# Low parts of weight chunks 7 to 41: a negating copy on ScalarE and an accumulating DMA from GpSimd, for every second chunk of both mixes

## The chip, the core and the metric

The kernel runs on one core of a Trainium2 chip. The time is that of one execution on the device in microseconds; of several runs the median is given. The engines are TensorE (PE in the profile), VectorE (DVE), ScalarE (ACT), GpSimd (POOL) and SyncE (SP, which here only issues DMAs). Each engine works through its own instructions in the order in which they stand; semaphores hold an instruction back until what it needs is done.

## The reference

A decoder trunk of two layers on 512 tokens of 1024 features, in fp32. Each layer is a token mix and a convolutional feed-forward block:

```python
def token_mix(h, ...):
    z = h @ w_in + b_in
    u_pool, u_conv, q, k, v, qi, ki, wi, gates = split_cols(z, IN_SIZES)
    ...
    y_pool = pool_mixer(u_pool, pool_w, pool_scale) @ w_pool_out
    y_conv = conformer_conv(u_conv, conv_dw_w, conv_dw_b, conv_ln_g, conv_ln_b, w_conv_out)
    y_attn = dsa_attention(q, k, v, qi, ki, wi) @ w_attn_out
    g = jax.nn.sigmoid(gates.astype(jnp.float32)).reshape(B, L, N_BRANCH, D_MODEL).astype(h.dtype)
    merged = g[:, :, 0] * y_pool + g[:, :, 1] * y_conv + g[:, :, 2] * y_attn
    return merged @ w_o

def reference(x, positions, ...):
    h = layer_norm(x, ln_in_g, ln_in_b)
    for l in range(DEPTH):
        mix = token_mix(h, positions, w_in[l], ...)
        h = layer_norm(DEEPNORM_ALPHA * h + mix, ln1_g[l], ln1_b[l])
        ffn = conv_ffn(h, w_up[l], ffn_dw_w[l], ffn_dw_b[l], w_down[l])
        h = layer_norm(DEEPNORM_ALPHA * h + ffn, ln2_g[l], ln2_b[l])
    return h
```

The mix has three branches. The pooling branch averages over windows of 2 to 16 tokens. The convolution branch filters 256 channels with 31 taps over time. The attention branch has an indexer (eight heads of relu logits, summed with weights) that chooses 128 of the visible keys for each query, and then rotary attention over those.

## The kernel before

**Weights.** All weights come from DRAM as chunks of 128 partitions x 1024 fp32 (512 KB), 123 for each layer, in the order of use. A chunk is split into two fp32r numbers (fp32 rounded to the format that TensorE takes): `w_hi`, the rounded value, and `w_lo`, what is left. Activations are split in the same way. A product is then three matmuls into one bank: hi x hi (L289), lo of the activation (L290), lo of the weight (L291). A chunk of the input projection holds 8 blocks of 128 rows, so it is 24 matmuls of 512 columns.

`Weights.emit` makes a chunk: SyncE issues its DMA into `w_raw` (L70, two buffers), ScalarE rounds it into `w_hi` (L74), and VectorE subtracts, `w_lo` = raw - hi (L78). Of the chunks in `side` (24, 26 to 40 of each mix, and some elsewhere) GpSimd subtracts instead, in two halves. `w_hi` and `w_lo` have four buffers each. `take` hands out the next chunk, and has the chunks up to two further ones (`look`) made.

**The mix.** Chunks 0 to 2 of a layer belong to its head (indexer keys, attention keys, the first half of the pooling channels), 3 to 6 to the indexer's queries, 7 to the second half of the pooling channels, 8 to 11 to the convolution's input, 12 to the values, 13 to 16 to the attention queries, 17 to 44 to the gates and the outputs of pooling and convolution, 45 to 56 to the attention's output and the merged output. Chunks 57 to 122 are the feed-forward block's.

Beside the projections run generators, of which some steps are taken after each chunk: the indexer (`index_gen`), whose logits TensorE puts into the two banks `pb_s` (L475, L476), ScalarE empties them into one of three `u` (L478), and VectorE adds them up in `pb_v` (L483) and then finds the largest (L490, L491); the pooling (L516 to L526 on GpSimd, L528 to L531 on VectorE); and the convolution (`conv_gen`). The latter works in two halves of 128 channels. ScalarE scales 23 of a half's taps (L595, two buffers `cvt`), GpSimd adds each to `cv` (L596); VectorE does the other seven into a bank `pb_p` (L598, L601) and adds both at the end (L604), which also frees that bank. There are two `pb_p`; the projection of chunk 16 (attention query tile 3) takes one of them.

Rotary embedding (`rotate`, `swapped`) copies a tile on ScalarE (L413), swaps its quarters by four SyncE DMAs (L405), multiplies on GpSimd (L407) and adds on VectorE (L417). `stack` splits the result (L424 ScalarE, L112 VectorE).

The order of instructions on each engine is decided when the program is built, by a scheduler with its own estimate of durations; work that is marked `high_priority` is put ahead of other work that is ready at the same time. Engines then keep this order on the chip.

Of the kernel before, what the change touches and what calls it, by code (L numbers as in the profile page):

```python
# [11 lines left out]
AF = mybir.ActivationFunctionType  # L12
ALU = mybir.AluOpType
# [30 lines left out]
N_CHUNK = 123  # L44
NSPLIT = {"mix": 3, "ffn": 3}
LAG = 2
MIX_SIDE = range(24, 42, 2)
ISSUE_ORDER = mybir.DependencyInfo(mybir.DependencyClass.NoSync, mybir.DependencyReason.DATA)
SIDE = 4
LN_POOL = ()  # L50
# [4 lines left out]
class Weights:  # L55
    def __init__(self, tc, w, raw_pool, split_pool, look, nchunk):
        self.tc, self.nc, self.w = tc, tc.nc, w
        self.raw_pool, self.split_pool = raw_pool, split_pool
        self.look = look
        self.n = nchunk  # L60
        self.emitted = 0
        self.used = 0
        self.ready = []
        self.side = set()

    def emit(self, upto):
        nc = self.nc
        while self.emitted < min(upto, self.n):
            raw = self.raw_pool.tile([P, D], F32, name="w_raw", tag="w_raw")
            nc.sync.dma_start(out=raw, in_=self.w[self.emitted])  # L70
            hi = self.split_pool.tile([P, D], F32R, name="w_hi", tag="w_hi")
            lo = self.split_pool.tile([P, D], F32R, name="w_lo", tag="w_lo")
            with self.tc.high_priority():
                nc.scalar.activation(hi, raw, AF.Copy)  # L74
                eng = nc.gpsimd if self.emitted in self.side else nc.vector
                for c in range(2 if self.emitted in self.side else 1):
                    cs = slice(512 * c, 512 * c + 512) if self.emitted in self.side else slice(0, D)
                    eng.tensor_tensor(out=lo[:, cs], in0=raw[:, cs], in1=hi[:, cs].bitcast(F32),  # L78
                                      op=ALU.subtract)
            self.ready.append((hi, lo))  # L80
            self.emitted += 1

    def take(self, look=None):
        self.emit(self.used + 1 + (self.look if look is None else look))
        self.used += 1
        return self.ready.pop(0)

# [2 lines left out]
def trunk_kernel(ctx, tc, x, positions, w, poolw, params, lnv, cons, out):  # L90
    nc = tc.nc
# [9 lines left out]
    W = Weights(tc, w, raw_pool, split_pool, 2, DEPTH * N_CHUNK)  # L101
# [203 lines left out]
    def down_proj(nk, lhs, ln, head):  # L305
# [3 lines left out]
        for s in range(2):  # L309
# [11 lines left out]
            def finish(b):  # L321
                hv = h[:, b, s * 512:(s + 1) * 512]
                V.scalar_tensor_tensor(out=hv, in0=hv, scalar=ALPHA, in1=po[b],
                                       op0=ALU.mult, op1=ALU.add)
                norm.stats(b, s)
                if s == 1:
                    norm.apply(b)
# [11 lines left out]
            if nt:  # L339
                wts = [W.take(look=nt - 1 - i) for i in range(nt)]  # L340
                W.emit(W.used + 4 - nt)
                for b in range(NB):
                    for i in range(nt):
                        for a in range(2):
                            first = mm(b, wts[i], npair - nt + i, a)
                            if i == a == 0 and b >= LAG and norm.tr[b - LAG] is not None:
                                tc.add_manual_dep(first.ins, norm.tr[b - LAG].ins.name, ISSUE_ORDER)
                    finish(b)
# [6 lines left out]
    def mix(l, head, prev, ln, nxt):  # L355
        es = ExitStack()
        with es:
# [5 lines left out]
            def q_slot(tag, dt=F32R):  # L363
                return slot(tag, {"qa": 6, "qb": 4, "qc": 4}[tag], dt)
# [7 lines left out]
            def p_slot(dt=F32):  # L372
                return slot("part", 9, dt, [P, 528])
# [9 lines left out]

            bga, bgb = [], []
            W.side.update(l * N_CHUNK + i for i in MIX_SIDE)

            def pump(q, n):
                while q and n > 0:
                    try:
                        n -= next(q[0])  # L390
                    except StopIteration:
                        q.pop(0)
# [366 lines left out]
            for jt in range(KT):  # L759
# [8 lines left out]
                hi, lo = q_slot("qa" if jt < 6 else "qb"), p_slot(F32R)[:, 0:L]  # L768
# [47 lines left out]
    for l in range(DEPTH):  # L816
        ffn_head = new_head("ffn")
        norm = mix(l, mix_head, norm, (1 + 2 * l, False), ffn_head)
        last = l == DEPTH - 1
        mix_head = None if last else new_head("mix")  # L820
        norm = ffn(l, ffn_head, norm, (2 + 2 * l, last), mix_head)
# [99 lines left out]
```

## Time and profile before

| | |
|---|---|
| median of 3 runs | 1506.07 us (1505.48 to 1506.64) |
| profiled execution | 1506.84 us, of which its span is 1505.0 us |
| mean granted TensorE clock | 0.994 |
| TensorE / VectorE / ScalarE / GpSimd busy | 97% / 63% / 45% / 35% |
| w_lo on VectorE (L78) | 210 times, 285.9 us |
| w_hi on ScalarE (L74) | 246 times, 260.6 us |
| w_lo halves on GpSimd (L78) | 72 times, 98.4 us |
| chain that ended last | TensorE 78%, GpSimd 8%, VectorE 6% of the span |

The profile is one execution, with the start and end of each instruction. The busy share of an engine is an average over the whole program; the mixes, the feed-forward blocks and the ends of the layers are loaded differently. The span runs from the first to the last instruction; 1.84 us of the execution lie outside it. In the rows "<-" behind an idle time names the instruction that released the waiting one.

### The profile page before, as it was taken

To read this page: it belongs to the slowest core of one execution; us is meant where nothing else is said; L and a number is where in the kernel's file an instruction comes from. 1 tells how busy PE (TensorE), PEld (TensorE's weight loads), DVE (VectorE), ACT (ScalarE), POOL (GpSimd) and SP (SyncE) were. 2 spreads that over 40 slices of the span, in tenths; PEclk is the share of its full clock that TensorE was granted. 3 is DMA by queue.
4 is the path that set the end of the run, shared out by engine and by line. 5 is a ranking of instruction groups with operands and counts; after the bars stand their busy time and mean duration, and the time that the engine had idled before them with its cause. 6 is when DMAs were issued, how large, how long until landed. Compare 5 with 4: busy or idle time off the path is not lost.

```text
span 1505.0 us, 18629 instructions
## 1 busy us (share of the span) xinstructions
PE 1454.7 (97%) x6850; PEld 1210.9 (80%) x6850; DVE 949.4 (63%) x1600; ACT 681.5 (45%) x1064; POOL 520.4 (35%) x395
## 2 busy tenths in 40 slices
PE   5998999999999999999999989999999999999997
PEld 5886888887878888888898768888878788888885
DVE  6789997645666555523267999865565655554234
ACT  5677455532544444421256874554235444443110
POOL 2458632237471111100134894220747311111004
PEclk9999999999999999999999999999999999999999
DMA  4432232232233333333224323222324333333331
GB/s 151 132 108 76 88 97 70 72 109 78 94 114 97 98 98 98 98 98 99 84 90 144 92 64 98 84 71 70 112 71 140 112 98 98 98 98 98 99 97 57
DMA packets 45019, 145.02 MB, mean 96 GB/s; under 512 B 6144, under 2 KB 7808, under 8 KB 44928
## 3 DMA queue, kind: packets, MB, share of 16 engines
q1 hardware_dynamic: 41472, 138.27, 29.6%
q10 hardware_dynamic: 3456, 5.57, 1.2%
q8 instruction: 54, 0.88, 0.2%
q14 instruction: 37, 0.30, 0.1%
HBM read 137.00 MB, written 2.10 MB: 92 GB/s over the span
## 4 chain that ended last, share of the span: by engine, by line
PE 78%; POOL 8%; DVE 6%; issue 3%; ACT 2%; DMA 2%; SPq 0%; POOLq 0%; ACTq 0%; DVEq 0%
PE pb_a L289 17%; PE pb_a L290 17%; PE pb_a L291 17%; POOL h L221 3%; POOL h L220 3%; PE pb_a L318 2%; PE pb_a L317 2%; PE pb_a L316 2%; PE pb_p L318 2%; PE pb_p L317 2%; PE pb_p L316 2%; PE pb_s L316 2%; PE pb_s L318 2%; PE pb_s L317 2%; POOL part L767 1%
## 5 line engine op out<-in xcount | busy, mean ns | idle before, releaser
L78 DVE TENSOR_TENSOR w_lo<-w_raw,w_hi 128x1024 fp32r<-128x1024 f32 x210 | 285.9, 1362 | 363.3 <-ACT w_hi L74 362.6
L289 PE MATMUL pb_a<-hT_hi,w_hi 128*128 128x512 f32 (+1 forms) x1200 | 468.4, 390 | 3.3 <-DVE fu L798 2.7
L291 PE MATMUL pb_a<-hT_hi,w_lo 128*128 128x512 f32 (+1 forms) x1200 | 468.2, 390 | 0.0
L290 PE MATMUL pb_a<-hT_lo,w_hi 128*128 128x512 f32 (+1 forms) x1200 | 467.6, 390 | 0.0
L74 ACT ACTIVATE w_hi<-w_raw 128x1024 fp32r<-128x1024 f32 x246 | 260.6, 1059 | 427.1 <-PE pb_a L290 203.5
L289 PEld LDWEIGHTS pb_a<-hT_hi,w_hi 128*128 128x128 f32 x1200 | 225.4, 188 | 48.3 <-ACT fu L795 3.5
L291 PEld LDWEIGHTS pb_a<-hT_hi,w_lo 128*128 128x128 f32 x1200 | 225.4, 188 | 44.6
L290 PEld LDWEIGHTS pb_a<-hT_lo,w_hi 128*128 128x128 f32 x1200 | 225.4, 188 | 44.3
L78 POOL TENSOR_TENSOR w_lo<-w_raw,w_hi 128x512 fp32r<-128x512 f32 x72 | 98.4, 1389 | 296.9 <-ACT w_hi L74 285.2
L804 POOL TENSOR_TENSOR fu<-fu 128x512 f32<-128x512 f32 x44 | 61.2, 1392 | 356.5 <-DVE fu L798 356.5
L596 POOL TENSOR_TENSOR cv<-cv,cvt 128x512 f32<-128x512 f32 x92 | 135.7, 1476 | 40.7 <-ACT cvt L595 35.0
L595 ACT ACTIVATE cvt<-cv,par 128x512 f32<-128x512 f32 x92 | 65.5, 720 | 21.9 <-POOL cv L596 21.5
L803 ACT ACTIVATE fu<-fu 128x512 f32<-128x512 f32 x44 | 27.8, 632 | 81.7 <-DVE fu L798 81.6
L798 DVE SCALAR_TENSOR_TENSOR fu<-pb_a,par,fu 128x510 f32<-128x510 f32 x82 | 61.4, 749 | 2.7
L795 ACT ACTIVATE fu<-pb_a,par 128x512 f32<-128x512 f32 x82 | 62.5, 762 | 0.0
L796 DVE SCALAR_TENSOR_TENSOR fu<-pb_a,par,fu 128x511 f32<-128x511 f32 x82 | 61.0, 743 | 0.0
L220 POOL TENSOR_TENSOR h<-h,gbt 128x512 f32<-128x512 f32 x32 | 50.9, 1622 | 19.8 <-DMA gbt<-in_lnv_dram 19.8
L687 ACT ACTIVATE qa<-qa,mx 128x128 f32<-128x128 f32 (+3 forms) x64 | 35.7, 559 | 42.3 <-DVE mx L684 41.1
L208 ACT ACTIVATE gbt<-pb_a,par 128x128 f32<-128x128 f32 x96 | 35.7, 467 | 40.0 <-PE pb_a L200 40.0
L490 DVE MAX8 m<-mask 128x8 f32<-128x256 f32 (+2 forms) x96 | 52.9, 555 | 1.1
L491 DVE MATCH_REPLACE8 mask<-m,mask 128x256 f32<-128x256 f32 (+2 forms) x96 | 52.1, 544 | 0.1
L316 PE MATMUL pb_a<-w_hi,g_hi 128*128 128x512 f32 x132 | 51.3, 389 | 0.0
(310 smaller groups left out, 2596.7 us busy)
## 6 DMA issues: line engine op xcount, KB each, us to landing
w_raw<-in_w_dram SPq DMA_DIRECT2D x246, 512.0 KB, 3.6
gbt<-in_lnv_dram ACTq DMA_DIRECT2D x20, 256.0 KB, 3.7
h<-in_x_dram SPq DMA_DIRECT2D x4, 512.0 KB, 5.5
t<-t SPq DMA_DIRECT2D x32, 64.0 KB, 2.0
out_dram<-h SPq DMA_DIRECT2D x8, 256.0 KB, 2.0
part<-t SPq DMA_DIRECT2D x32, 48.0 KB, 2.2
part<-t SPq DMA_DIRECT2D x16, 64.0 KB, 2.0
par<-in_params_dram SPq DMA_DIRECT2D x2, 143.5 KB, 6.5
```

The lines of the kernel that those rows point to most:

```text
L74: nc.scalar.activation(hi, raw, AF.Copy)
L78: eng.tensor_tensor(out=lo[:, cs], in0=raw[:, cs], in1=hi[:, cs].bitcast(F32), op=ALU.subtract)
L220: G.tensor_tensor(out=hb, in0=hb, in1=gb[0][c], op=ALU.mult)
L289: T.matmul(o, wh, xh(xc), start=(i == 0), stop=False)
L290: T.matmul(o, wh, xl(xc), start=False, stop=False)
L291: T.matmul(o, wl, xh(xc), start=False, stop=(i == n - 1))
L316: first = T.matmul(po[b], lh(k, b), wh, start=(k == 0), stop=False)
L317: T.matmul(po[b], lh(k, b), wl, start=False, stop=False)
L318: T.matmul(po[b], ll(k, b), wh, start=False, stop=(k == nk - 1))
L595: A.activation(tm, hp[c][:, i:i + L], AF.Copy, scale=tap(i))
L596: G.tensor_tensor(out=pacc, in0=pacc, in1=tm, op=ALU.add)
L795: A.activation(t, o, AF.Identity, bias=par[:, l, PO_FB + ct:PO_FB + ct + 1], scale=tapw(2))
```

## The change

For chunks 7, 9, ... 41 of each mix (`MIX_DMA`, 18 in a layer) `w_lo` is made in another way. ScalarE writes `w_lo` = -raw, rounded (new L77). GpSimd issues an accumulating DMA that adds the same chunk, read from DRAM a second time, to it (new L78), so that raw - rounded raw is left. ScalarE's `w_hi` is the same copy as before (new L79). VectorE's subtraction is left out. When the chunk after the look-ahead is such a chunk, `take` has one chunk more made. All other chunks are made as before, at new L84 and L88. Behind the class, lines move by 12 or 13: L289 to L291 are new L301 to L303, L407 is L420, L483 is L496, L516 to L526 are L529 to L539, L573 is L586, L596 is L609.

```diff
--- before.py
+++ after.py
@@ -45,6 +45,7 @@
 NSPLIT = {"mix": 3, "ffn": 3}
 LAG = 2
 MIX_SIDE = range(24, 42, 2)
+MIX_DMA = range(7, 42, 2)
 ISSUE_ORDER = mybir.DependencyInfo(mybir.DependencyClass.NoSync, mybir.DependencyReason.DATA)
 SIDE = 4
 LN_POOL = ()
@@ -62,6 +63,7 @@
         self.used = 0
         self.ready = []
         self.side = set()
+        self.by_dma = set()
 
     def emit(self, upto):
         nc = self.nc
@@ -70,6 +72,14 @@
             nc.sync.dma_start(out=raw, in_=self.w[self.emitted])
             hi = self.split_pool.tile([P, D], F32R, name="w_hi", tag="w_hi")
             lo = self.split_pool.tile([P, D], F32R, name="w_lo", tag="w_lo")
+            if self.emitted in self.by_dma:
+                with self.tc.high_priority():
+                    nc.scalar.activation(lo, raw, AF.Copy, scale=-1.0)
+                    nc.gpsimd.dma_start(out=lo, in_=self.w[self.emitted], accum_op=ALU.add)
+                    nc.scalar.activation(hi, raw, AF.Copy)
+                self.ready.append((hi, lo))
+                self.emitted += 1
+                continue
             with self.tc.high_priority():
                 nc.scalar.activation(hi, raw, AF.Copy)
                 eng = nc.gpsimd if self.emitted in self.side else nc.vector
@@ -81,7 +91,9 @@
             self.emitted += 1
 
     def take(self, look=None):
-        self.emit(self.used + 1 + (self.look if look is None else look))
+        if look is None:
+            look = self.look + (self.used + self.look + 1 in self.by_dma)
+        self.emit(self.used + 1 + look)
         self.used += 1
         return self.ready.pop(0)
 
@@ -383,6 +395,7 @@
 
             bga, bgb = [], []
             W.side.update(l * N_CHUNK + i for i in MIX_SIDE)
+            W.by_dma.update(l * N_CHUNK + i for i in MIX_DMA)
 
             def pump(q, n):
                 while q and n > 0:
```

The scheduler's order changes too. On GpSimd, in layer 0, from the last rotations of the indexer's queries (L407, new L420) through the pooling's second half (L516 and L523 to L526, new L529 and L536 to L539) to the convolution's taps (L596, new L609); before:

```order
L407 TENSOR_TENSOR part<-part,sinT 128x384
L516 TENSOR_TENSOR part<-part 128x527
L523 TENSOR_TENSOR part<-part 128x525
L524 TENSOR_TENSOR part<-part 128x521
L525 COPY part<-part 64x512
L526 TENSOR_TENSOR part<-part 64x512
L596 TENSOR_TENSOR cv<-cv,cvt 128x512 x14
L407 TENSOR_TENSOR t<-t,sinT 128x512
```

and in the change, where "DMA w_lo" is the accumulating DMA (the two together are those of chunks 11 and 13, the next ones of 15 and 17):

```order
L420 TENSOR_TENSOR part<-part,sinT 128x384 x2
L78 DMA w_lo<-in_w_dram 128x1024 x2
L529 TENSOR_TENSOR part<-part 128x527
L536 TENSOR_TENSOR part<-part 128x525
L537 TENSOR_TENSOR part<-part 128x521
L538 COPY part<-part 64x512
L539 TENSOR_TENSOR part<-part 64x512
L609 TENSOR_TENSOR cv<-cv,cvt 128x512 x2
L78 DMA w_lo<-in_w_dram 128x1024
L609 TENSOR_TENSOR cv<-cv,cvt 128x512 x7
L78 DMA w_lo<-in_w_dram 128x1024
L609 TENSOR_TENSOR cv<-cv,cvt 128x512 x3
L420 TENSOR_TENSOR t<-t,sinT 128x512
```

The two issues now stand ahead of the pooling's second half, and two more between the first taps of the convolution; a third follows 17 taps into that half.

On VectorE, in layer 0, around the pooling's second half (the second L528, new L541) and the two halves of the convolution's input (L573, new L586); before:

```order
L528 SCALAR_TENSOR_TENSOR u<-part,cst 128x512
L78 TENSOR_TENSOR w_lo<-w_raw,w_hi 128x1024
L483 SCALAR_TENSOR_TENSOR pb_v<-u,wq,pb_v 128x256
L530 TENSOR_TENSOR u<-part,cst 128x16
L531 TENSOR_TENSOR u<-u,part 128x16
L112 TENSOR_TENSOR part<-u,part 128x512
L78 TENSOR_TENSOR w_lo<-w_raw,w_hi 128x1024 x2
L573 SCALAR_TENSOR_TENSOR cv<-t 128x512
L528 SCALAR_TENSOR_TENSOR u<-part,cst 128x512
L483 SCALAR_TENSOR_TENSOR pb_v<-u,wq,pb_v 128x256
L530 TENSOR_TENSOR u<-part,cst 128x16
```

and in the change:

```order
L541 SCALAR_TENSOR_TENSOR u<-part,cst 128x512
L543 TENSOR_TENSOR u<-part,cst 128x16
L544 TENSOR_TENSOR u<-u,part 128x16
L496 SCALAR_TENSOR_TENSOR pb_v<-u,wq,pb_v 128x256
L124 TENSOR_TENSOR part<-u,part 128x512
L88 TENSOR_TENSOR w_lo<-w_raw,w_hi 128x1024
L586 SCALAR_TENSOR_TENSOR cv<-t 128x512
L541 SCALAR_TENSOR_TENSOR u<-part,cst 128x512
L543 TENSOR_TENSOR u<-part,cst 128x16
L544 TENSOR_TENSOR u<-u,part 128x16
L496 SCALAR_TENSOR_TENSOR pb_v<-u,wq,pb_v 128x256
L586 SCALAR_TENSOR_TENSOR cv<-t 128x512
```

Two of three w_lo rows (L78, new L88) are gone from this piece; the second half of the pooling (L541) now stands ahead of the second half of the convolution's input as before.

On TensorE, in layer 0, ahead of the projection that takes the bank `pb_p` (chunk 16), with the last logits (L475, L476, new L488, L489) and the first attention scores (L680, L681, new L693, L694); before:

```order
L475 MATMUL pb_s<-qa,qb 128x512
L476 MATMUL pb_s<-qa,qb 128x512
L475 MATMUL pb_s<-qa,qb 128x512
L476 MATMUL pb_s<-qa,qb 128x512
L680 MATMUL pb_s<-qc,qa_hi 128x128
L681 MATMUL pb_s<-qc,qa_hi 128x128
L680 MATMUL pb_s<-qc,qa_hi 128x128
L681 MATMUL pb_s<-qc,qa_hi 128x128
L289 MATMUL pb_p<-hT_hi,w_hi 128x512
```

and in the change:

```order
L488 MATMUL pb_s<-qa,qb 128x512
L489 MATMUL pb_s<-qa,qb 128x512
L488 MATMUL pb_s<-qa,qb 128x512
L489 MATMUL pb_s<-qa,qb 128x512
L693 MATMUL pb_s<-qc,qa_hi 128x128
L694 MATMUL pb_s<-qc,qa_hi 128x128
L693 MATMUL pb_s<-qc,qa_hi 128x128
L694 MATMUL pb_s<-qc,qa_hi 128x128
L693 MATMUL pb_s<-qc,qa_hi 128x128
L694 MATMUL pb_s<-qc,qa_hi 128x128
L301 MATMUL pb_p<-hT_hi,w_hi 128x512
```

Three pairs of scores instead of two now stand ahead of this projection.

## Rows read from the trace of the kernel before

**Rows 1.** Busy time of the engines, from the page's head and part 1.

```profile
span 1505.0 us, 18629 instructions
...
PE 1454.7 (97%) x6850; PEld 1210.9 (80%) x6850; DVE 949.4 (63%) x1600; ACT 681.5 (45%) x1064; POOL 520.4 (35%) x395
```

**Rows 2.** Slices: us, each engine's busy time (instructions), granted clock, DMA share, GB/s.

```profile
125.00:150.00 25.00, 19.62 (x72) 14.68 (x72) 24.65 (x56) 20.00 (x36) 22.25 (x17) 0.86 0.23 72
150.00:175.00 25.00, 25.00 (x113) 20.64 (x112) 24.17 (x48) 15.66 (x22) 23.17 (x16) 1.00 0.29 98
850.00:875.00 25.00, 19.83 (x76) 14.95 (x75) 24.59 (x43) 20.16 (x33) 21.35 (x17) 0.86 0.30 85
```

**Rows 3.** TensorE's timeline: start, length, line, tiles, idle time before it and releaser.

```profile
131.45 0.51 PE L475 MATMUL pb_s<-qa,qb 128*128 128x512 f32 x1 [1.84 <-ACT u L478]
...
135.76 0.80 PE L289 MATMUL pb_p<-hT_hi,w_hi 128*128 128x512 f32 x1 [0.30 <-DVE cv L604]
...
140.97 0.40 PE L289 MATMUL pb_p<-hT_hi,w_hi 128*128 128x512 f32 x1
...
868.16 0.80 PE L475 MATMUL pb_s<-qa,qb 128*128 128x512 f32 x1 [2.48 <-ACT u L478]
```

**Rows 4.** ScalarE's timeline, one row inside the first place.

```profile
130.80 0.60 ACT L478 ACTIVATE u<-pb_s 128x512 f32<-128x512 f32 x1 [1.08 <-DVE pb_v L483]
```

**Rows 5.** Slice up to the last wait of layer 0, columns as in rows 2.

```profile
84.00:136.00 52.00, 45.84 (x200) 36.36 (x199) 48.95 (x92) 42.08 (x70) 41.89 (x29) 0.98 0.33 99
```

**Rows 6.** VectorE's L78 in both stretches: ns least/median/most, first and last start.

```profile
L78 DVE TENSOR_TENSOR w_lo<-w_raw,w_hi x8: 1210/1222/2274, 82.8 to 127.8; 128x1024 fp32r<-128x1024 f32 x8
...
L78 DVE TENSOR_TENSOR w_lo<-w_raw,w_hi x6: 1206/1576/1919, 827.4 to 864.4; 128x1024 fp32r<-128x1024 f32 x6
```

**Rows 7.** GpSimd's timeline in both stretches, filter taps (L596).

```profile
92.58 3.96 POOL L596 TENSOR_TENSOR cv<-cv,cvt 128x512 f32<-128x512 f32 x2 [0.18 <-ACT cvt L595]
...
108.12 4.98 POOL L596 TENSOR_TENSOR cv<-cv,cvt 128x512 f32<-128x512 f32 x3 [0.29 <-ACT cvt L595]
...
127.67 1.29 POOL L596 TENSOR_TENSOR cv<-cv,cvt 128x512 f32<-128x512 f32 x1
...
131.13 3.88 POOL L596 TENSOR_TENSOR cv<-cv,cvt 128x512 f32<-128x512 f32 x3
...
842.73 4.89 POOL L596 TENSOR_TENSOR cv<-cv,cvt 128x512 f32<-128x512 f32 x3 [0.64 <-ACT cvt L595]
```

**Rows 8.** GpSimd's waits, 84:136 and 820:873 us: total, times, longest.

```profile
POOL cv L596 <- ACT cvt L595: 15.5, 7, 13.0
...
POOL cv L596 <- ACT cvt L595: 17.2, 10, 11.5
```

**Rows 9.** DMA issues of the page (median us to landing), and one of SyncE's issues.

```profile
w_raw<-in_w_dram SPq DMA_DIRECT2D x246, 512.0 KB, 3.6
...
t<-t SPq DMA_DIRECT2D x32, 64.0 KB, 2.0
...
56.95 0.33 SPq L70 DMA_DIRECT2D w_raw<-in_w_dram  x1
```

**Rows 10.** Timelines of ScalarE, GpSimd and TensorE around chunk 7 of layer 0.

```profile
56.81 1.06 ACT L74 ACTIVATE w_hi<-w_raw 128x1024 fp32r<-128x1024 f32 x1
...
57.18 1.02 POOL L407 TENSOR_TENSOR part<-part,sinT 128x384 f32<-128x384 f32 x1 [3.86 <-DMA part<-t]
...
61.59 0.40 PE L291 MATMUL pb_a<-hT_hi,w_lo 128*128 128x512 f32 x1
```

**Rows 11.** Timelines of GpSimd (pooling), ScalarE (chunk 13) and VectorE, layer 0.

```profile
69.10 1.06 POOL L516 TENSOR_TENSOR part<-part 128x527 f32<-128x527 f32 x1
...
75.10 1.28 POOL L526 TENSOR_TENSOR part<-part 64x512 f32<-64x512 f32 x1
...
81.73 1.04 ACT L74 ACTIVATE w_hi<-w_raw 128x1024 fp32r<-128x1024 f32 x1
...
87.35 0.75 DVE L528 SCALAR_TENSOR_TENSOR u<-part,cst 128x512 f32<-128x512 f32 x1
```

## The prediction

> **What bounds the kernel now.** I read the page's busy line first: TensorE works 1454.7 of a span of 1505.0 us [rows 1], so only time in which TensorE stands still or runs slowly can come back. Cut into slices of 25 us, the mixes show where that is. The slice from 150 us holds 113 matmuls in 25.00 us, 0.221 us each; the one from 125 us holds 72 and the one from 850 us holds 76, at a mean granted clock of 0.86 [rows 2]. The 41 and 37 missing ones are 9.1 and 8.2 us: about 17 us are the most that can come back in these two places, and the rest of the mixes has little.
>
> TensorE's timeline of the first place has a string of waits, the longest 1.84 us at 131.45, the last 0.30 us at 135.76. Then twelve matmuls take 5.21 us, from 135.76 to 140.97 [rows 3]; at 0.221 us they are 2.65, so 2.6 us go to the lower of the clock's two levels, granted right after those waits. Layer 1 has its longest wait, 2.48 us, at 868.16 [rows 3].
>
> What ends the waits: the logits of the attention indexer wait for ScalarE to empty a PSUM bank (`u`, L478). ScalarE itself had waited 1.08 us for VectorE, which had not used up the `u` before (L483) [rows 4]. The last wait ends when VectorE adds up the first half of the convolution (L604) [rows 3]. VectorE is busy 48.95 of the 52 us up to there, ScalarE 42.08, GpSimd 41.89 [rows 5]. So VectorE is late, and its queue holds weight subtractions that the change takes out. But L604 also needs the filter taps that GpSimd adds one after another, and the last three of those end at 131.13 + 3.88 = 135.01 [rows 7], 0.75 us before TensorE goes on. **Two chains end together**; shortening VectorE's alone moves nothing.
>
> **The change, part by part.** 36 subtractions leave VectorE, 18 in each mix. Where TensorE is not held up this is worth nothing; chunks 15, 17 and 19 lie in the two held-up stretches. At the medians of 1.222 and 1.576 us [rows 6], three are 3.7 us in layer 0 and 4.7 in layer 1. This is VectorE's relief, and the gain if nothing else were late.
>
> GpSimd's relief. Undisturbed, one of its tensor operations takes 1.29 us; beside a w_lo, two took 3.96 and three 4.98 us in layer 0, three 4.89 us in layer 1 [rows 7]. Over the undisturbed price that is 1.38 + 1.11 = 2.5 us in layer 0 and 1.0 us in layer 1, which come back with the removed w_lo. GpSimd also waited for ScalarE's scaled taps: 15.5 us, of which 13.0 are before the first tap, so 2.5 us in layer 0's chain, and 17.2 - 11.5 = 5.7 us in layer 1's [rows 8]. ScalarE was late partly because of VectorE, but it gets a second pass of 1.06 us over every odd chunk while only 10 of 52 us are free. I take half of these waits as saved, 1.25 and 2.85 us (bounds: none, all).
>
> GpSimd's new load. Three of the DMA issues stand between the taps of that first half. This trace has no GpSimd issue; the nearest rows are SyncE's issue of a chunk, 0.33 us [rows 9], and GpSimd's own operation, 1.29 us [rows 7]. Nothing speaks for either end, so I take about the middle, 0.85 us: 2.55 us in each layer (1.0 to 3.9).
>
> Net on the tap chain: layer 0 -2.5 - 1.25 + 2.55 = -1.2 us, layer 1 -1.0 - 2.85 + 2.55 = -1.3 us. VectorE gains more in both, so the tap chain decides, and these are the terms. The half-speed stretch stays, as its waits do.
>
> The first accumulated chunk. The w_hi of chunk 7 is made from 56.81 to 57.87; the negating copy behind it ends at 58.93, and GpSimd's rotation ahead of the issue ends before, at 58.20 [rows 10]. Then 0.85 for the issue and a landing. No accumulating transfer is in the trace; the plain one of the same 512 KB takes 3.6 us [rows 9], which I take: the data is there at 63.4. TensorE first reads this w_lo at 61.59 [rows 10]: **+1.8 us**. Bounds: nothing, with 0.33 and the 2.0 us of the shortest kind of transfer [rows 9] (61.3), and 5.4 us if the sum costs as much as two transfers. In layer 1, I count nothing for it: the same steps, worked out there, end before the first read.
>
> The trace does not show how an addition in the DMA is paid. The page "Collectives: The Full Stack" of the Trainium skill, section "The bandwidth ceiling: the fold count and why AG ≠ RS ≠ AR", says that a reduction needs two source reads where a copy needs one, and so runs at about half the rate. That speaks for the upper bound, and the sum by it would be 3.6 us higher.
>
> Chunk 13 in layer 0. Its issue stands ahead of five pooling operations that ran from 69.10 to 76.38 [rows 11], and GpSimd's queue keeps its order until the negated copy is there. With w_hi at 81.73 to 82.77 as before, 1.06 for negating and 0.85 for the issue, the five begin at 84.7 and end at 92.0, where VectorE took their result (L528) at 87.35 [rows 11]: 4.6 us late, with the second half of the convolution's input queued behind. But one more chunk of look-ahead lets w_hi begin when chunk 9 is off TensorE, at about 78, an estimate from the chunks' pace, and then the result is in time within a microsecond. Between 0 and 4.6 I take **+1.0 us**, nearer the earlier start.
>
> Later chunks: a pair of buffers is handed over three chunks ahead of its use, 3 x 24 x 0.221 = 15.9 us. Two passes on ScalarE, the issue and a landing of 3.6 to 7.2 us make 6.6 to 10.2 us; the rest is room for standing in GpSimd's queue. I take no stall; what it costs without that cover is the third rival. The extra 36 x 512 KB meet DMA engines that are a third busy in the fullest stretch [rows 5]. The three score pairs instead of two that TensorE does before its bank only fill its wait.
>
> **Sum:** -1.2 - 1.3 + 1.8 + 1.0 = +0.3 us. The profiled execution took 1506.84 us, 1.84 of it outside the span, and lies 0.77 above the median of 1506.07. 1506.84 + 0.3 - 0.77 = 1506.4, rounded to **1506 us**: no change that can be told, since a measurement of this kernel tells about 0.2% (3 us) from none.
>
> **Rivals.**
> Faster: GpSimd's issues fall into gaps in which it waited anyway, so that VectorE's relief decides. 3.7 + 4.7 = 8.4 us come back; where the shorter waits keep the clock up, 2.6 us per layer on top, 13.6 in all. Less 1.8 for chunk 7, that is 1494 to 1499.5; say 1497. For it: 8.2 us of such gaps in the two chains [rows 8]. Against: ScalarE, which causes the gaps, gets more work. It decides where an issue costs GpSimd less than 0.4 us net.
>
> Slower, by GpSimd's queue: an issue that comes to its head before the negated copy is made holds up the taps behind it. If it waits for the two passes of ScalarE (2.1 us) and then costs 1.3, three cost 10.2 us instead of 2.55, 7.6 more in each layer: 1521; with half of such waits, and in one layer, 1510. Say 1513. From (2.5 + 1.25) / 3 = 1.25 us per issue in layer 0 and 1.3 in layer 1 the tap chain gets longer than before. For it: ScalarE is 81% busy in this stretch. Against: its copies are placed with priority.
>
> Slower, by late data: an issue that stands behind five taps at 1.66 us (three in 4.98 [rows 7]) and lands 7.2 us later needs 2.1 + 8.3 + 0.85 + 7.2 = 18.5 of the 15.9 us. Three such chunks are 7.8 us, and 3.6 more at chunk 7: 1518; with the slow landing at chunk 7 alone 1510. The double landing of the Trainium skill's page above is this case. For it: an addition has to read what is there. Against: past the taps GpSimd's queue is short of work.
>
> **How the numbers follow.** Even trade (1500 to 1511) 0.38; VectorE's relief 0.29; GpSimd's queue 0.19; late data 0.14. Of the even trade 0.28 lies within 0.2%, 0.06 below and 0.04 above. Faster 0.29 + 0.06 = 0.35; same 0.28; slower 0.19 + 0.14 + 0.04 = 0.37. The range holds 8 in 10: it goes from the faster rival's lower half to the middle of the slower ones, 1494 to 1517 us; the likeliest case's own is 1500 to 1511.
>
> **What would show it.** Right: TensorE waits for the w_lo of chunk 7 by 1 to 3 us in layer 0, and for none in layer 1; the tap chain of the first half takes 1 us less than before, though VectorE has gaps in it; the waits before 136 and 868 us, and the low clock behind them, are there still. Wrong in the sum: a GpSimd issue far from 0.85 us, or a landing far from 3.6 us. Wrong altogether: TensorE waits for w_lo at several odd chunks, GpSimd stands idle ahead of its issues, or the low clock is gone from both places. The price of the issue and the landing time, which no row shows, make the prediction wrong most easily.

## The result and the profile after

The changed kernel takes 1535.77 us (median of 5 runs, 1533.38 to 1536.22) against 1506.64 us of the kernel before in the same series: a ratio of 1.0187, 95% interval 1.0176 to 1.0198. By the ratio it is slower by about 28 us, outside the range of the prediction. The profiled execution took 1534.93 us, with a span of 1533.1 us.

From the page after: the head and part 1, and the DMA issues of part 6 (size, median us from issue to landing).

```profile
span 1533.1 us, 18706 instructions
...
PE 1461.6 (95%) x6850; PEld 1213.9 (79%) x6850; DVE 911.9 (59%) x1564; ACT 712.2 (46%) x1100; POOL 530.1 (35%) x431
...
w_raw<-in_w_dram SPq DMA_DIRECT2D x246, 512.0 KB, 3.6
w_lo<-in_w_dram POOLq DMA_DIRECT2D x36, 512.0 KB, 7.7
...
t<-t SPq DMA_DIRECT2D x32, 64.0 KB, 6.3
...
part<-t SPq DMA_DIRECT2D x32, 48.0 KB, 4.7
```

VectorE is 37 us less busy, ScalarE 31 us more (36 second passes); both were meant. The two new things stand in part 6. The accumulating transfer lands after 7.7 us, and the swaps of the rotary embedding, t<-t, which took 2.0 us before [rows 9], take 6.3. The 48 KB swaps went from 2.2 to 4.7 us.

TensorE's waits in the whole program after (total, times, longest):

```profile
PE pb_a L303 <- DMA w_lo<-in_w_dram: 11.0, 3, 5.3
PE pb_s L488 <- ACT u L491: 10.6, 8, 4.0
...
PE pb_a L301 <- DVE qa_lo L124: 3.0, 2, 1.8
...
PE pb_p L301 <- DVE vst L124: 2.1, 2, 1.3
```

Three waits are for accumulated low parts: one of 2.65 us at chunk 23 of layer 0, one of 3.01 us at chunk 7 and one of 5.34 us at chunk 23 of layer 1. The others shown are old ones, longer (7.6, 1.0 and 1.6 us before). Where did the time go? I compared the starts of the matmuls with a low weight part (L291, after L303), the first of before with the first of after and so on, and noted where the distance grows. (A few records are missing, so single values are good to about half a microsecond.)

```
layer 0  chunk 7        +1.5      layer 1  chunk 7        +3.4
         chunk 9        +1.1               chunk 9        +2.0
         109 to 142 us  +6.6               850 to 877 us  +4.0
         chunk 23       +3.4               chunk 23       +8.2
         rest           -1.2               rest           -1.2
         sum           +11.4               sum           +16.4
```

Chunk 23 of both layers and chunk 7 of layer 1 are where TensorE waits for accumulated data. In layer 0 it does not wait for that of chunk 7: it does matmuls of chunk 8 first, so the +1.5 is counted early, and behind both chunks the distance is 0.2 us. Chunk 9 and the middle stretches hold none of these waits either. At chunk 9 of layer 1 TensorE waits 1.80 us for ScalarE, which had waited 3.01 us for a chunk's load: SyncE issued it at 813.88, 0.7 us behind an accumulation, and it took 8.4 us to land instead of 3.6.

In the middle stretches the rotations are late. One such chain in layer 0, from GpSimd through ScalarE to TensorE:

```profile
135.12 1.27 POOL L420 TENSOR_TENSOR t<-t,sinT 128x512 f32<-128x512 f32 x1 [2.25 <-DMA t<-t]
...
137.64 0.72 ACT L608 ACTIVATE cvt<-cv,par 128x512 f32<-128x512 f32 x1 [3.04 <-POOL cv L609]
...
138.75 1.06 ACT L491 ACTIVATE u<-pb_s 128x512 f32<-128x512 f32 x2
...
139.38 0.80 PE L488 MATMUL pb_s<-qa,qb 128*128 128x512 f32 x1 [3.99 <-ACT u L491]
```

GpSimd waits for a swap, ScalarE's next filter tap waits for GpSimd to free a buffer, the emptying of an indexer bank (`u`) stands behind that tap, and TensorE waits 3.99 us for it; its longest wait here before was 1.84 us [rows 3].

The slices of the middle stretches and of chunk 23 in layer 1, columns as in [rows 2]:

```profile
125.00:150.00 25.00, 15.94 (x53) 11.09 (x52) 21.70 (x53) 19.99 (x37) 19.96 (x17) 0.80 0.35 85
875.00:900.00 25.00, 18.23 (x65) 12.63 (x64) 22.75 (x54) 21.36 (x35) 19.62 (x16) 0.86 0.32 85
925.00:950.00 25.00, 22.86 (x92) 18.79 (x93) 20.29 (x49) 11.21 (x16) 13.88 (x13) 0.86 0.54 128
```

The slice from 125 us holds 53 matmuls instead of 72 [rows 2], with VectorE less busy than before, 21.70 instead of 24.65. The one from 925 us has a low clock that the kernel before had nowhere near it: it follows the wait for chunk 23. The DMA engines are busy 0.32 to 0.54 of the time, so a mean share far under one did not keep small transfers from taking three times as long.

One chain of timeline rows, layer 1, from SyncE, GpSimd, ScalarE, GpSimd and TensorE in this order, shows how the two costs hang together:

```profile
902.31 3.47 SPq L418 DMA_DIRECT2D t<-t  x4
...
911.20 1.29 POOL L420 TENSOR_TENSOR t<-t,sinT 128x512 f32<-128x512 f32 x1 [4.02 <-DMA t<-t]
...
913.78 0.72 ACT L608 ACTIVATE cvt<-cv,par 128x512 f32<-128x512 f32 x1 [5.56 <-POOL cv L609]
...
917.84 1.05 ACT L77 ACTIVATE w_lo<-w_raw 128x1024 fp32r<-128x1024 f32 x1
...
919.31 0.87 POOL L78 DMA_DIRECT2D w_lo<-in_w_dram  x1
...
927.14 0.80 PE L303 MATMUL pb_a<-hT_hi,w_lo 128*128 128x512 f32 x1 [5.34 <-DMA w_lo<-in_w_dram]
```

The swaps are issued right behind chunk 21's accumulation, which GpSimd issued at 902.00; GpSimd can go on with them at 911.20. GpSimd stood idle for 4.02 us, with filter taps queued behind. ScalarE's next scaled tap has no free buffer until GpSimd goes on, 5.56 us. The negated copy of chunk 23 stands behind that in ScalarE's queue; it comes at 917.84, its transfer is issued at 919.31 and ends TensorE's wait 7.8 us later, at 927.14.

### The profile page after: what moved, and what is told of

Same layout as the page of the kernel before. It is cut to its first block, busy times and chain, and to the rows that moved or that the text cites. A ratio compares the mean times of both kernels' runs of the same rounds, so it can differ in the third digit from the quotient of the medians.

```text
span 1533.1 us, 18706 instructions
## 1 busy us (share of the span) xinstructions
PE 1461.6 (95%) x6850; PEld 1213.9 (79%) x6850; DVE 911.9 (59%) x1564; ACT 712.2 (46%) x1100; POOL 530.1 (35%) x431
## 4 chain that ended last, share of the span: by engine, by line
PE 71%; POOL 9%; DMA 7%; ACT 5%; issue 3%; DVE 3%; SPq 1%; ACTq 0%; POOLq 0%; DVEq 0%
PE pb_a L303 15%; PE pb_a L301 15%; PE pb_a L302 15%; POOL h L233 3%; POOL h L232 3%; DMA t<-t 2%; DMA w_raw<-in_w_dram 2%; PE pb_a L330 2%; PE pb_a L329 2%; PE pb_a L328 2%; PE pb_p L328 2%; PE pb_p L329 2%; PE pb_p L330 2%; PE pb_s L328 1%; PE pb_s L329 1%
## 5 line engine op out<-in xcount | busy, mean ns | idle before, releaser
L303 PE MATMUL pb_a<-hT_hi,w_lo 128*128 128x512 f32 (+1 forms) x1200 | 469.6, 391 | 11.3 <-DMA w_lo<-in_w_dram 11.0
L301 PE MATMUL pb_a<-hT_hi,w_hi 128*128 128x512 f32 (+1 forms) x1200 | 469.1, 391 | 6.4 <-DVE fu L811 2.3
L88 DVE TENSOR_TENSOR w_lo<-w_raw,w_hi 128x1024 fp32r<-128x1024 f32 x174 | 235.6, 1354 | 358.5 <-ACT w_hi L84 358.2
L84 ACT ACTIVATE w_hi<-w_raw 128x1024 fp32r<-128x1024 f32 x210 | 222.7, 1061 | 412.3 <-PE pb_a L302 191.0
L303 PEld LDWEIGHTS pb_a<-hT_hi,w_lo 128*128 128x128 f32 x1200 | 226.0, 188 | 56.4 <-DMA w_lo<-in_w_dram 11.5
L301 PEld LDWEIGHTS pb_a<-hT_hi,w_hi 128*128 128x128 f32 x1200 | 226.1, 188 | 53.5 <-ACT fu L808 3.1
L88 POOL TENSOR_TENSOR w_lo<-w_raw,w_hi 128x512 fp32r<-128x512 f32 x72 | 95.7, 1349 | 269.4 <-ACT w_hi L84 259.7
L609 POOL TENSOR_TENSOR cv<-cv,cvt 128x512 f32<-128x512 f32 x92 | 123.2, 1340 | 16.2 <-ACT cvt L608 11.8
L78 POOL DMA_DIRECT2D w_lo<-in_w_dram x36 | 31.8, 884 | 108.2 <-ACT w_lo L77 102.5
L79 ACT ACTIVATE w_hi<-w_raw 128x1024 fp32r<-128x1024 f32 x36 | 38.0, 1055 | 35.5 <-PE pb_a L302 15.2
```

Of the source, the lines that this page charges most:

```text
L301: T.matmul(o, wh, xh(xc), start=(i == 0), stop=False)
L303: T.matmul(o, wl, xh(xc), start=False, stop=(i == n - 1))
L609: G.tensor_tensor(out=pacc, in0=pacc, in1=tm, op=ALU.add)
```

## The experiments

Theory A: the accumulating transfers cost, by landing late and by holding up the swaps. Theory B: GpSimd's queue, ScalarE's second pass and the new order cost, whatever the transfer does. All runs are set against the kernel before on the same chip (medians 1507.5 to 1508.5 us there). Only run 1 keeps the order of all instructions of the change on the four computing engines, as its trace shows. Every other edit also changes the order that the scheduler makes, and runs 8 and 11 show that a change without any transfer of its own can cost 4 to 5 us; differences of that size between the other runs tell little.

**1. A plain transfer.** Leaves out the addition; the low part is the raw weight.

```diff
-nc.gpsimd.dma_start(out=lo, in_=self.w[self.emitted], accum_op=ALU.add)
+nc.gpsimd.dma_start(out=lo, in_=self.w[self.emitted])
```

> The transfer writes the chunk over the negated copy instead of adding to it (so the low part is the raw weight); same bytes written, same order of all instructions. Theory A (what costs is the added transfer itself: its 7.7 us landing, and the swaps and rotations that it holds up): a plain one should land in about 4 us and the swaps in 3 to 4 us instead of 6.3, so most of the 29 us come back, 1508 to 1516 us. Theory B (what costs is GpSimd's queue, ScalarE's second pass and the new order): nothing of that changes, 1530 to 1536 us.

Measured: 1516.29 us, ratio 1.0054 (1.0039 to 1.0068). Its DMA issues:

```profile
w_lo<-in_w_dram POOLq DMA_DIRECT2D x36, 512.0 KB, 5.0
...
t<-t SPq DMA_DIRECT2D x32, 64.0 KB, 4.5
```

With the same order of every instruction and the same passes, some 20 of the 28 us are gone when the transfer does not add. This is the clearest single result. One thing besides the transfer changed: an issue keeps GpSimd busy for 0.58 us instead of 0.88, so a small part of the 20 us may belong to GpSimd's queue. The other 8 us are what theory B can claim beyond that, and part of those belongs to the transfer that is left (64 KB swaps at 4.5 us, 48 KB swaps still at 4.8, two waits for w_lo of 3.4 us in all).

**2. An eighth of the columns.** Leaves out the addition for columns 128 to 1023.

```diff
-nc.gpsimd.dma_start(out=lo, in_=self.w[self.emitted], accum_op=ALU.add)
+nc.gpsimd.dma_start(out=lo[:, 0:128], in_=self.w[self.emitted][:, 0:128], accum_op=ALU.add)
```

> Only columns 0 to 127 of a chunk are accumulated (64 KB instead of 512), the rest of the low part stays the negated copy. Issues and second passes stay. Theory A: no wait for w_lo, swaps back near 2 us, 1500 to 1510 us. Theory B: 1526 to 1536 us.

Measured: 1510.83 us, ratio 1.0022 (1.0012 to 1.0031). The 64 KB accumulations land in 4.1 us and the swaps in 3.5, not near 2, and one wait for w_lo of 1.5 us is left. The run lies just beyond the upper end of A. All 36 subtractions are gone from VectorE, the traffic nearly so, and the kernel is still not faster than before. ScalarE's second pass is still in it; set against run 8, which has that pass and keeps the subtractions (3.8 us), this run's loss of 3.3 us leaves no gain by VectorE's relief that can be told.

**3. The late chunks only.**

```diff
-MIX_DMA = range(7, 42, 2)
+MIX_DMA = range(25, 42, 2)
```

> Only chunks 25 to 41 take the new way. Theory A: no rotation runs there and no wait for w_lo was seen there, so no change to before, 1504 to 1509 us. Theory B: half of the issues and passes stay, about 1518 to 1522 us.

Measured: 1507.71 us, ratio 0.9997 (0.9988 to 1.0007). Accumulations at 7.4 us, 18 of them, cost nothing where no rotation runs and three chunks of time lie ahead of the use. Swaps stay at 2.0 us. As A has it.

**4. Three chunks apart from the swaps.**

```diff
-MIX_DMA = range(7, 42, 2)
+MIX_DMA = (11, 13, 15)
```

> Only chunks 11, 13 and 15 take the new way; their transfers lie between the swaps of the indexer's queries and those of the attention queries. Theory A: no loss, 1503 to 1508 us. Theory B: three of 18 issues, about 1511 us.

Measured: 1512.44 us, ratio 1.0030 (1.0019 to 1.0041). A missed this: the swaps are at 2.0 us, no low part is late, and 4.7 us are lost, which is nearer to what B had. Run 11 bears on it.

**5. Without chunks 7 and 23.**

```diff
-MIX_DMA = range(7, 42, 2)
+MIX_DMA = tuple(i for i in range(7, 42, 2) if i not in (7, 23))
```

> Chunks 7 and 23, at which TensorE waited for the accumulated low part, go the old way; the other 16 of a layer the new one. Theory A, first half (data that land late cost about 16 of the 29 us, the delays at these two chunks in both layers): 1517 to 1522 us, with no wait of TensorE for an accumulation; the swaps still land in about 6 us. If the swaps and rotations alone were the cause: 1530 to 1536 us. Theory B (queue, passes, order): about 1532 us.

Measured: 1516.49 us, ratio 1.0061 (1.0045 to 1.0078); one wait of TensorE for an accumulated low part is left, 0.5 us, and the swaps are at 5.8 us. The two chunks account for some 19 us, a little more than expected.

**6 and 7. Without the swaps.** Both kernels multiply the unswapped tile; the rotation's small transfers are left out.

```diff
-for r in range(4):
-    nc.sync.dma_start(out=sw[32 * r:32 * r + 32, 0:n],
-                      in_=t[32 * (r ^ 1):32 * (r ^ 1) + 32, 0:n])
-G.tensor_tensor(out=sw[:, 0:n], in0=sw[:, 0:n], in1=sinT[:, c0:L], op=ALU.mult)
+G.tensor_tensor(out=sw[:, 0:n], in0=t[:, 0:n], in1=sinT[:, c0:L], op=ALU.mult)
```

> The changed kernel without the quarter swaps of the rotary embedding: GpSimd multiplies the unswapped tile, and SyncE's small transfers are left out. To be set against the kernel before with the same left out (next run). Theory A, second half (slow swaps make the middle of the mix late, some 10 to 12 us): only the late low parts at chunks 7 and 23 stay, so 13 to 18 us more than the next run. Theory B, or slow swaps without effect: 25 to 30 us more.

> The kernel before without the quarter swaps, the base for the run above. They land in 2 us there and little waits for them: 1498 to 1508 us by every theory.

Measured: the change without swaps 1506.43 us (ratio 0.9995, 0.9985 to 1.0004), the kernel before without swaps 1501.18 us (0.9959, 0.9944 to 0.9974). The change costs 5.3 us here instead of 28, less than the 13 to 18 expected, though its accumulations still land in 7.5 us. TensorE's wait for them:

```profile
PE pb_a L303 <- DMA w_lo<-in_w_dram: 1.1, 2, 0.8
```

So the low parts are hardly late either. Most of that lateness was then not the landing alone, but the late start that the chain above shows: without slow swaps GpSimd and ScalarE come to chunk 23 in time. (The landing has its share: at chunk 7 of layer 1 it took 9.1 us.) This is why taking out chunks 7 and 23 (19 us) and taking out the swaps (23 us) together give more than the whole loss.

**8. The second pass alone.** VectorE's subtraction stays and overwrites the negated copy. The cut is shown against the kernel before; the look-ahead of the change is in it too.

```diff
+if self.emitted in self.by_dma:
+    nc.scalar.activation(lo, raw, AF.Copy, scale=-1.0)
 nc.scalar.activation(hi, raw, AF.Copy)
 eng = nc.gpsimd if self.emitted in self.side else nc.vector
```

> The second pass of ScalarE and the extra look-ahead alone: the negated copy is written and then overwritten by VectorE's subtraction as before; no accumulating transfer. Theory A: the pass costs little, 1506 to 1512 us. Theory B with the pass as its main part: over 1518 us.

Measured: 1511.32 us, ratio 1.0025 (1.0016 to 1.0034): 3.8 us.

**9. The look-ahead alone.** As run 8, without the pass.

> Only the extra look-ahead of the change (one chunk more made when chunk 7, 9, ... 41 is next); the split is as in the kernel before. If the 3.8 us of the second pass alone came from ScalarE's time, this is the kernel before, 1505 to 1509 us; if they came from the new order and the earlier hand-out of buffers, 1509 to 1513 us.

Measured: 1507.72 us, ratio 0.9999 (0.9990 to 1.0009). The look-ahead is free, so the 3.8 us of run 8 come with the pass: its time, and the order that the scheduler makes around it. These two were not told apart.

**10. Three chunks at the swaps.**

```diff
-MIX_DMA = range(7, 42, 2)
+MIX_DMA = (17, 19, 21)
```

> Only chunks 17, 19 and 21 take the new way, those whose accumulation is issued at the swaps of the attention queries. Theory A (swaps held up): the swaps of these queries land in about 6 us, GpSimd and ScalarE wait for them as in the full change, and chunk 23 (now VectorE's) is not late: 1513 to 1519 us, more than the 1512 of chunks 11, 13 and 15. If the loss goes by the number of chunks only: 1510 to 1512 us, the same as for those three.

Measured: 1519.74 us, ratio 1.0070 (1.0053 to 1.0087). Its DMA issues, and GpSimd's rows that wait for swaps in layer 0:

```profile
w_lo<-in_w_dram POOLq DMA_DIRECT2D x6, 512.0 KB, 8.1
...
t<-t SPq DMA_DIRECT2D x32, 64.0 KB, 5.9
```

```profile
133.95 1.26 POOL L420 TENSOR_TENSOR t<-t,sinT 128x512 f32<-128x512 f32 x1 [3.43 <-DMA t<-t]
...
162.44 1.28 POOL L420 TENSOR_TENSOR t<-t,sinT 128x512 f32<-128x512 f32 x1 [4.02 <-DMA t<-t]
```

The new way for six chunks at the swaps costs 11.2 us, a little beyond what A had, and brings the swaps to 5.9 us in the median. For as many chunks that miss the swaps it costs 4.7. The pass alone on chunks 17, 19 and 21 was not run.

**11. The pass on chunks 11, 13 and 15 alone.** Run 8 with these three chunks.

> ScalarE's second pass and the look-ahead on chunks 11, 13 and 15 alone, subtraction on VectorE, no accumulation. If the 4.7 us of the run with these three chunks were ScalarE's pass and the order that the scheduler makes of it: 1510 to 1513 us. If they were the accumulations': 1506 to 1509 us.

Measured: 1513.30 us, ratio 1.0033 (1.0021 to 1.0045), the same total as run 4. The pass and the order that comes with it are thus enough for a loss of this size without any accumulation. That they are run 4's loss is not shown, as the two runs differ in order and in their waits. In this run TensorE's longest wait inside the layers' mixes is one of 4.8 us, for VectorE's `part` (L740), which no transfer of weights touches; the same wait in run 4 is 1.9 us, and others are longer there:

```profile
PE pb_a L295 <- DVE part L740: 4.8, 1, 4.8
```

**12 and 13. The swap on ScalarE**, computed in full, for the kernel before and for the change; this was also a try for a version better than both.

```diff
-t = t_slot()
-A.activation(t[:, 0:n], o[:, 0:n], AF.Identity, bias=bias)
+sw = slot_s()[:, 0:n]
+for r in range(4):
+    q = slice(32 * (r ^ 1), 32 * (r ^ 1) + 32)
+    A.activation(sw[32 * r:32 * r + 32], o[q, 0:n], AF.Identity, bias=bias[q])
...
-sw = swapped(t, c0, slot_s)
+G.tensor_tensor(out=sw, in0=sw, in1=sinT[:, c0:L], op=ALU.mult)
```

> The kernel before with the rotations' quarter swap as four 32-partition copies of ScalarE out of PSUM in place of one copy and four transfers (computes the same). Leaving the swaps out gave 6 us; the copies cost ScalarE some 1.8 us in each rotation. By the wait for the transfers alone 1501 to 1504 us; by ScalarE's load, as with the second pass, 1508 to 1514 us.

> The changed kernel with the same swap on ScalarE: all accumulations, issues and second passes stay, the whole result is computed, and no small transfer is left that an accumulation could hold up. Theory A: within 4 to 8 us of the run above, 1505 to 1518 us. If the accumulations cost by other ways than the swaps (late data, queue, order): 1525 us or more.

Measured: 1516.72 us (ratio 1.0061, 1.0046 to 1.0076) and 1525.50 us (1.0120, 1.0105 to 1.0135). ScalarE can't carry the swaps: 9 us lost, a little beyond the expected. On that base the change costs 8.8 us, slightly over the 4 to 8 that A had, against 28 with the swaps as transfers. The time itself, 1525.50 us, is where the other reading was put (1525 us or more); as the base came out later than assumed too, the difference is what counts, and some of it is late data (4.3 us of TensorE's waits for accumulated low parts). No version was found that beats the kernel before.

## Why the prediction was wrong

**The two chains.** That VectorE's relief moves nothing agrees with run 2: there it is in full, beside little traffic, and no gain can be told. In the change the middle stretches got longer although VectorE had less to do.

**GpSimd's load.** "I take about the middle, 0.85 us" held. The page after has it in part 5, with the taps:

```profile
L609 POOL TENSOR_TENSOR cv<-cv,cvt 128x512 f32<-128x512 f32 x92 | 123.2, 1340 | 16.2 <-ACT cvt L608 11.8
...
L78 POOL DMA_DIRECT2D w_lo<-in_w_dram x36 | 31.8, 884 | 108.2 <-ACT w_lo L77 102.5
```

An issue costs 0.884 us. A tap takes 1.34 us, and GpSimd waits for ScalarE's taps 11.8 us in all; the rows before had more of it inside the two chains and ahead of their first taps [rows 8]. These single terms had the right sign, and the net of the tap chain, 1.2 us less in layer 0, failed: VectorE adds up the first half (L604, new L617) at 142.54 instead of 135.04. The terms were for a chain that was not held from elsewhere, and GpSimd waited in it for the swaps, as the rows at 135.12 show.

**The landing of the accumulation.** The step "the plain one of the same 512 KB takes 3.6 us [rows 9], which I take" is the first that failed. From the start of the issue to the landing it took 7.7 us, where 0.85 and 3.6 make 4.45; the upper bound, 0.85 and twice 3.6, was nearly right. The page "Collectives: The Full Stack" of the Trainium skill, section "The bandwidth ceiling: the fold count and why AG ≠ RS ≠ AR", with its two source reads, was on the right side here: from the same queue a plain 512 KB landed in 5.0 us and an adding one in 7.7, a factor of 1.5. The time that its packets took in the DMA engines about doubled for the same bytes, as a share of the 16 engines' span (packets, MB, share), in the change and in run 1:

```profile
q0 software_dynamic: 5184, 18.88, 7.0%
...
q0 software_dynamic: 5184, 18.88, 3.6%
```

**Chunk 7.** In layer 0 a stall of 1.8 us for the accumulated data was forecast, and none came. The new order lets TensorE begin the next chunk before it needs chunk 7's low part, and its one wait there, 0.30 us, is for VectorE's low part of that next chunk:

```profile
60.48 0.39 PE L301 MATMUL pb_a<-hT_hi,w_hi 128*128 128x512 f32 x1
...
61.40 0.50 PE L301 MATMUL pb_a<-hT_hi,w_hi 128*128 128x512 f32 x1
...
62.66 0.50 PE L303 MATMUL pb_a<-hT_hi,w_lo 128*128 128x512 f32 x1 [0.30 <-DVE w_lo L88]
```

In layer 1, "I count nothing for it" failed. GpSimd issued the transfer at 802.90, it landed 9.1 us later, and TensorE, at its low part, waited until 812.00, 3.01 us:

```profile
812.00 0.50 PE L303 MATMUL pb_a<-hT_hi,w_lo 128*128 128x512 f32 x1 [3.01 <-DMA w_lo<-in_w_dram]
```

**Chunk 13.** The chain that the prediction described came as described: the issue at 83.89, and VectorE's L541 waits for the pooling until 91.75, near the late end of 92.0; the earlier start that the look-ahead was to give did not come. TensorE lost nothing by it, so +1.0 was near the truth by luck: the result was late by what the late end said, and nothing that TensorE needed hung on it.

```profile
91.75 0.75 DVE L541 SCALAR_TENSOR_TENSOR u<-part,cst 128x512 f32<-128x512 f32 x1 [1.18 <-POOL part L539]
```

**The extra traffic.** "The extra 36 x 512 KB meet DMA engines that are a third busy" is the step that cost most. It priced the mean share of the engines and not what a small transfer takes beside a large one. All 32 of the 64 KB swaps were issued while an accumulation was under way, and the trace shows that they wait it out: each landed between 1.9 us before and 1.9 us after the accumulation did, whether issued 0.3 or 6 us behind it. In run 1 the same holds with the earlier landing of the plain transfer: every swap landed behind it, by at most 1.7 us. The accumulations are hardly slowed by the swaps in turn, for without swaps (run 6) they still take 7.5 us. The swaps are few and small, but GpSimd, in order, waits for each, ScalarE waits for GpSimd's tap buffers, and negated copies wait behind ScalarE's. By run 7 against run 6, 23 of the 28 us go with the swaps, by runs 12 and 13 some 19. By runs 4 and 10, the new way for three chunks per layer costs 11.2 us at the swaps and 4.7 off them.

**Later chunks.** "I take no stall" failed at chunk 23 in both layers, 3.4 and 8.2 us with the low clock after the second. The rival "late data" had the place in GpSimd's queue as the cause; the chain of layer 1 showed ScalarE's queue instead, itself late by GpSimd, itself late by the swaps. At chunks 25 to 41 no stall was right (run 3).

**The second pass** had no term of its own. Run 8 prices it at 3.8 us, with the order that comes with it.

What stays open: why a swap waits out the GpSimd transfer ahead of it and does not pass it; how the 5 to 9 us that the change costs without swap transfers divide between the pass, its order and late data, beyond the 3.8 of run 8; and whether the 4.7 us of run 4 are the pass's.

## What to carry to other kernels

A transfer that is added off the critical path has to be priced by what it does to the small transfers beside it, and by who waits for those: here a mean DMA share of a third hid a tripling of a 2 us transfer that an in-order engine stands behind. An accumulating DMA is worth trying where its use lies far ahead and nothing small and urgent is in flight (run 3 lost nothing); a gain is to be looked for only where the engine that it relieves is alone in being late, which two chains that end together are not. Before moving work off a busy engine, test the relief with the replacement made nearly free; run 2, with an eighth of the traffic though with the second pass, showed no gain.

## What the runs showed of the hardware

A 512 KB transfer landed 3.6 us after SyncE's issue, 5.0 us after GpSimd's (plain), and 7.7 us after GpSimd's when it added to its destination; a 64 KB one that added took 4.1 us. Adding kept the DMA engines about twice as long for the same bytes, 7.0% of their span against 3.6% (run 1), and its issue kept GpSimd 0.88 us against 0.58. Beside adding transfers of 512 KB, SyncE's 64 KB swaps inside SBUF went from 2.0 to 6.3 us, beside plain ones of GpSimd's to 4.5, and beside adding ones of 64 KB still to 3.5: those issued behind a GpSimd transfer of 512 KB landed within 2 us of its landing. SyncE's 512 KB loads kept their median of 3.6 us, but 15 of 246 took over 5 us, against 4 before; one issued 0.3 us behind an accumulation took 8.6.
